# Expert fetches one at a time, query pieces loaded ahead, seven and then nine fetch buffers

## The chip, the cores and the metric

The kernel runs on one core of one Trainium2 chip. The metric is device time in microseconds (us) of one execution, the median of several. TensorE is PE, its weight loads are PEld, VectorE is DVE, ScalarE is ACT, GpSimd is POOL, and SyncE, which only issues loads and stores here, is SP. Each engine works through its own queue in order, and a queue whose head has to wait holds up everything behind it.

## The reference, cut to what matters

Two transformer blocks run over 256 tokens of width 1024. The first block is attention (a difference attention and a retention, side by side) and then a feed-forward layer of product-key experts; the second block follows and is not touched. What matters is the expert layer:

```python
def one_block(xb):                                    # 128 tokens; there are two such tiles
    q = (xb @ w_query).reshape(tb, 8, 2, 128)
    s = einsum('thpd,hpnd->thpn', q, sub_keys)        # 8 heads, 2 halves, 128 keys each
    top_s, top_i = top_k(s, 16)
    # all pairs of the two halves, 16 best pairs -> 16 expert numbers and gates a head
    best_s, pos = top_k(cand_s, 16)
    eid  = take_along_axis(cand_i, pos)
    gate = softmax(best_s)
    u = take(expert_down, eid)                        # rows of 1024
    act = gelu(einsum('thkd,td->thk', u, xb))
    v = take(expert_up, eid)                          # rows of 1024
    return einsum('thk,thkd->td', gate * act, v)
```

So each token fetches 128 experts (8 heads of 16), each a row of 1024 numbers for `u` and one of 1024 for `v`.

## The kernel before

`uv` in device memory holds the `u` row and the `v` row of each of the 16384 experts side by side. A fetch (line 753) is one indirect DMA from POOL: for one slot s of 128 it brings, for the 128 tokens of a tile, 128 rows of 8 KB, 1 MB in all. There are 2 x 128 fetches. A fetch buffer is a tile `uv` of the pool `up`; there are eight. For each fetch DVE forms the dot product of the `u` half with the normed token `xn` (line 756, to `dots`), ACT applies Gelu (759), multiplies by the gate (765) and spreads the result over a diagonal `dg` (767), and PE multiplies `dg` by the `v` half into two accumulators (770: two matmuls in the source, which run as four). Only then is the buffer free for a later fetch. `fetch` works in pairs: two fetches and two dots, then one Gelu over both, then the rest for the pair before in the source.

The expert numbers are found while the fetches run. `queries` multiplies by 16 pieces of `w_query` (512 KB each) and by the sub-keys `skT`; `picks` (its generator `choose` from line 632) does the two top-16 searches on DVE and one Exp on ACT for each unit of heads (line 680). Between fetches, `picking(time, t, h)` emits DVE steps until their estimated costs reach `time`; the table `due` forces a unit to be finished by a given slot. `behind()` keeps such DVE steps behind the dot of that slot in DVE's queue; it ties no other engine. `query(1)` or `memory(1)` emits half a head, or a piece of the memory block's weights, about every sixth slot.

A weight piece goes through `piece`: SP loads it (line 166, tile `raw`), ACT rounds it to `wh` (167), and DVE takes the rest `wl` (168). `raw`, `wh` and `wl` have three buffers each, in the pool `wp`, shared by all weights. So the load of a piece waits until DVE has done the `wl` of the piece three before, and its `wh` waits until PE is done with that piece.

The toolchain places instructions in each engine's queue by its own estimate of when they can run, so that a load or a rounding may stand ahead of its place in the source. Attention (`mix1`) lives in the pool `m1`, whose room the expert stage then reuses tile by tile; the expert stage opens `up2` when all queries are done. `skT` and `qT` lie in the pool `qp`, which closes then.

Of the kernel before, what the change touches and what calls it, by code (L numbers as in the profile page):

```python
# [15 lines left out]
OP = mybir.AluOpType  # L16
# [98 lines left out]
class K:  # L115
# [32 lines left out]
    def piece(self, src, shape, between=None):  # L148
# [3 lines left out]
        def t(tag, dt):  # L152
            x = self.wp.tile([128, 1024], dt, name=tag, tag=tag)
            x = x[:, :n]
            if len(shape) > 1:
                x = x.rearrange("p (a b) -> p a b", b=shape[-1]) if len(shape) == 2 else \
                    x.rearrange("p (a b c) -> p a b c", b=shape[1], c=shape[2])
            return x
# [152 lines left out]
    def mix1(self):  # L311
# [3 lines left out]
        with self.tc.tile_pool(name="m1", bufs=1, reuse_waits="tile") as mp:  # L315
# [90 lines left out]
            mix = M([128, 2, 1024], "mix")  # L406
            mT = (M([128, 8, 256], "mTh", F32R), M([128, 8, 256], "mTl", F32R))
# [7 lines left out]
            dif = mix[:, :, :512].rearrange("p t (h d) -> p t h d", d=128)  # L415
            ret = mix[:, :, 512:].rearrange("p t (h d) -> p t h d", d=128)
# [72 lines left out]
            fill(4)  # L489
            a = diff_turn(p)  # L490
# [19 lines left out]
            a = diff_turn(p)  # L510
            diff_out(3, a)
# [29 lines left out]
            def half(nb, k0):  # L541
# [4 lines left out]
                if k0:  # L546
                    self.squares(nb)
# [16 lines left out]
    def rope(self, v, g, half, cn, sn, M):  # L564
# [4 lines left out]
        a = M([128, 2, g, 64], "ropeA", bufs=1)[:, :, :, :2 * half]  # L569
        b = M([128, 2, g, 64], "ropeB", bufs=1)[:, :, :, :2 * half]  # L570
# [5 lines left out]
    def transposeN(self, x, nb, M, tag):  # L576

        nc = self.nc
        o = (M([128, nb, 256], tag + "h", F32R), M([128, nb, 256], tag + "l", F32R))
# [30 lines left out]
    def queries(self, pool, skT, sS):  # L610
# [3 lines left out]
        self.first_T([I["w_query"][b] for b in range(2)], two, self.pv("ffn_g", 0, 8))  # L614
        self.r = self.res_r()
        for h in range(8):
            qT = pool.tile([128, 2, 256], F32, name="qT", tag="qT", bufs=2)
            for i in range(2):
                o = two[i]
                if h:  # L620
                    o = self.pa([128, 256])
                    self.proj_T(self.hT, self.piece(I["w_query"][2 * h + i], [8, 128]), 8, o)
# [63 lines left out]
    def experts(self):  # L686
# [4 lines left out]
        with self.tc.tile_pool(name="p2", bufs=1, reuse_waits="tile") as p2, \  # L691
# [15 lines left out]
            xn = [P([1024], f"xn{t}") for t in range(2)]  # L707
            for t in range(2):
                nc.gpsimd.dma_start(xn[t], I["ffn_gr"].to_broadcast([128, 1024]))
# [8 lines left out]
            units = [(0, h, 1) for h in range(4)] + [(0, 4, 2), (0, 6, 2), (1, 0, 4), (1, 4, 4)]  # L718
# [21 lines left out]

            def fetch(t, acc):
# [3 lines left out]
                last = None  # L745
                for s in range(0, 130, 2):
                    new = None
                    if s < 128:
                        rows = []
                        dots = up.tile([128, 2], F32, name="dots", tag="dots", bufs=4)  # L750
                        for i in range(2):
                            x = up.tile([128, 2048], F32, name="uv", tag="uv", bufs=8)
                            nc.gpsimd.indirect_dma_start(x, None, I["uv"],  # L753
                                                         bass.IndirectOffsetOnAxis(ap=eids[:, s + i:s + i + 1], axis=0))
                            junk = self.junk([128, 1024], "junk", BF)
                            self.dot = nc.vector.scalar_tensor_tensor(junk, x[:, :1024], 1.0, xn[t], op0=OP.mult,  # L756
                                                                      op1=OP.mult, accum_out=dots[:, i:i + 1])
                            rows.append(x)
                        nc.scalar.activation(dots, dots, AF.Gelu, scale=self.r[:, t:t + 1])  # L759
                        new = s, rows, dots  # L760
                    if last:
                        s0, rs, ds = last
                        dg = up.tile([128, 2, 128], F32, name="dg", tag="dg", bufs=3)
                        for i in range(2):
                            nc.scalar.activation(ds[:, i:i + 1], ds[:, i:i + 1], AF.Copy,  # L765
                                                 scale=gates[:, s0 + i:s0 + i + 1])
                            nc.scalar.activation(dg[:, i], self.ident, AF.Copy, scale=ds[:, i:i + 1])  # L767
                        for i in range(2):
                            for d in range(2):
                                nc.tensor.matmul(acc[d], dg[:, i], rs[i][:, 1024 + 512 * d:1536 + 512 * d],  # L770
                                                 start=s0 + i == 0, stop=s0 + i == 127)
                    last = new
                    yield s
# [4 lines left out]
            due = {8: (0, 2), 24: (0, 3), 40: (0, 4), 56: (0, 6), 88: (0, 8), 120: (1, 4)}  # L778
            with self.tc.tile_pool(name="qp", bufs=1, reuse_waits="tile") as qp:
# [12 lines left out]
                for s in tile0:  # L792
                    with behind():
                        if s in (2, 6, 10) or s > 10 and s % 6 == 4:
                            query(1)
                            n += 1
                        picking(1500, 0, min(8, (n + 1) // 2))
# [4 lines left out]
                query.rest()  # L802
            with self.tc.tile_pool(name="up2", bufs=1, reuse_waits="tile") as up2:
                self.fg = up2.tile([128, 1024], F32, name="fgr")
                nc.sync.dma_start(self.fg, I["final_g"].to_broadcast([128, 1024]))
                self.xg = [up2.tile([128, 512], F32, name=f"xg{t}") for t in range(2)]
                for s in tile0:
                    with behind():
                        if s % 6 == 4:
                            self.memory(1)  # L810
                        picking(1500, 1, 8)
# [873 lines left out]
```

## Time and profile before

| | |
|---|---|
| median of 3 runs | 1339.29 us (1338.74 to 1340.62) |
| profiled execution, its own time | 1340.03 us |
| its span in the profile | 1338.0 us |
| mean granted TensorE clock | 0.960 of full speed |
| busy share of the span: PE, DVE, ACT, POOL | 88%, 70%, 47%, 24% |
| fetches `uv`, from first issue to last landing | 147.7 to 865.4 us |

The profiled execution's own time is 2.0 us over its span, and 0.7 us over the median. The profile puts a busy time, a count and an idle time with its releaser beside each group of instructions; a busy PE is not a PE at its peak, since matmuls are pipelined and their ends modelled. Device memory traffic is given as GB/s and as a busy share of the core's 16 DMA engines.

### The profile page before, as it was taken

Reading aid. Unit: us, or ns where it says so; the run is one execution under the profiler, and the core shown is the slowest. Engines: PE = TensorE matmul, PEld = TensorE weight load, DVE = VectorE, ACT = ScalarE, POOL = GpSimd, SP = SyncE. Lnnn points to the kernel's source line nnn. Section 1 sums busy time; section 2 is a strip of 40 time slices with the busy share of each in tenths; the row PEclk is TensorE's granted clock in tenths of the full one; section 3 lists DMA queues with packets and bytes.
Section 4 is the critical chain, followed back from the end, with each engine's and each line's share of the span. In section 5 each row is a group of like instructions: output and inputs, shape, how many; then the busy total and the mean of one; then the engine's idle time right before and its main releaser. Section 6 shows DMA issues by size and latency. Waiting matters only on the chain.

```text
span 1338.0 us, 16678 instructions
## 1 busy us (share of the span) xinstructions
PE 1171.0 (88%) x5430; PEld 807.6 (60%) x5430; DVE 936.2 (70%) x2188; ACT 633.4 (47%) x1501; POOL 315.5 (24%) x283
## 2 busy tenths in 40 slices
PE   7999688979688988879877777789999999999996
PEld 5877554545344444344432223279987898999996
DVE  6888678575777776555545455478987885988887
ACT  6676434333332423423322222257877575655554
POOL 0020334434244544334443333110001000000001
PEclk9999798989899999989999999999999999999998
DMA  7645599999999999999999999846334464656562
GB/s 261 227 140 174 231 361 400 406 371 420 373 371 395 406 420 410 359 411 422 421 422 422 420 422 420 342 130 190 122 106 127 131 215 142 192 188 181 185 188 95
DMA packets 81769, 388.61 MB, mean 290 GB/s; under 512 B 8196, under 2 KB 10324, under 8 KB 48788
## 3 DMA queue, kind: packets, MB, share of 16 engines
q0 software_dynamic: 37408, 270.56, 49.6%
q1 hardware_dynamic: 42260, 114.38, 26.3%
q10 hardware_dynamic: 2016, 2.62, 0.5%
q8 instruction: 43, 0.70, 0.2%
q14 instruction: 42, 0.34, 0.1%
HBM read 384.38 MB, written 3.15 MB: 290 GB/s over the span
## 4 chain that ended last, share of the span: by engine, by line
PE 38%; DMA 31%; issue 13%; DVE 9%; POOL 5%; ACT 3%; POOLq 0%; SPq 0%; ACTq 0%; DVEq 0%
DMA uv<-in_uv_dram,eid 27%; PE pa L173 5%; PE pa L174 5%; PE pa L175 5%; POOL uv L753 5%; PE pb L173 4%; PE pa L1514 4%; PE pb L175 4%; PE pb L174 4%; DVE junk L756 3%; PE pb L770 2%; DVE wl L168 2%; DMA raw<-in_w_query_dram 1%; DMA raw<-in_w_mem_k_dram 1%; DMA raw<-in_w_in_dram 1%
## 5 line engine op out<-in xcount | busy, mean ns | idle before, releaser
L770 PE MATMUL pb<-uv,dg 128*128 128x512 f32 x1024 | 495.5, 632 | 100.5 <-ACT dg L767 100.3
L756 DVE SCALAR_TENSOR_TENSOR junk<-uv,xn 128x1024 bf16<-128x1024 f32 x256 | 313.4, 1224 | 239.8 <-DMA uv<-in_uv_dram,eid 229.3
L770 PEld LDWEIGHTS pb<-uv,dg 128*128 128x128 f32 x1024 | 198.4, 202 | 358.2 <-issue 198.6
L753 POOL DMA_INDIRECT uv<-in_uv_dram,eid x256 | 286.5, 1119 | 451.4 <-PE pb L770 303.3
L167 ACT ACTIVATE wh<-raw 128x1024 fp32r<-128x1024 f32 (+3 forms) x203 | 211.9, 1047 | 367.1 <-DMA raw<-in_w_mem_v_dram 51.4
L168 DVE TENSOR_TENSOR wl<-raw,wh 128x1024 fp32r<-128x1024 f32 (+3 forms) x203 | 246.7, 1219 | 60.2 <-ACT wh L167 59.7
L759 ACT ACTIVATE dots<-dots,rs_y 128x2 f32<-128x2 f32 x128 | 37.3, 292 | 240.1 <-DVE junk L756 236.8
L173 PE MATMUL pb<-nTh,wh 128*128 128x256 f32 x416 | 117.7, 283 | 0.0
L174 PE MATMUL pb<-nTl,wh 128*128 128x256 f32 x416 | 117.7, 283 | 0.0
L175 PE MATMUL pb<-nTh,wl 128*128 128x256 f32 x416 | 117.4, 283 | 0.0
L767 ACT ACTIVATE dg<-cvt,dots 128x128 f32<-128x128 f32 x256 | 86.9, 386 | 0.0
L175 PE MATMUL pa<-nTh,wl 128*128 128x256 f32 x256 | 78.0, 305 | 5.6 <-DVE wl L168 5.6
L173 PE MATMUL pa<-nTh,wh 128*128 128x256 f32 x256 | 78.2, 306 | 4.5 <-ACT wh L167 4.4
L174 PEld LDWEIGHTS pb<-nTl,wh 128*128 128x128 f32 x416 | 79.5, 191 | 1.0
L173 PEld LDWEIGHTS pb<-nTh,wh 128*128 128x128 f32 x416 | 79.5, 191 | 1.0
L175 PEld LDWEIGHTS pb<-nTh,wl 128*128 128x128 f32 x416 | 79.5, 191 | 0.0
L1538 POOL TENSOR_TENSOR xs<-xr,ng 128x512 f32<-128x512 f32 x4 | 5.1, 1290 | 313.9 <-DVE xr L1536 313.9
L174 PE MATMUL pa<-nTl,wh 128*128 128x256 f32 x256 | 73.6, 288 | 0.0
L173 PE MATMUL pa<-wh,nTh 128*128 128x512 f32 (+1 forms) x144 | 58.2, 412 | 9.8 <-ACT wh L167 9.0
L765 ACT ACTIVATE dots<-dots,gate 128x1 f32<-128x1 f32 x256 | 61.5, 286 | 4.0
L174 PE MATMUL pa<-wl,nTh 128*128 128x512 f32 (+1 forms) x144 | 58.1, 403 | 3.2 <-DVE wl L168 3.2
L175 PE MATMUL pa<-wh,nTl 128*128 128x512 f32 (+1 forms) x144 | 57.5, 400 | 0.0
(460 smaller groups left out, 1895.2 us busy)
## 6 DMA issues: line engine op xcount, KB each, us to landing
raw<-in_w_ffn_up_dram SPq DMA_DIRECT2D x44, 512.0 KB, 3.7
raw<-in_w_out_dram SPq DMA_DIRECT2D x24, 512.0 KB, 3.7
raw<-in_w_in_dram SPq DMA_DIRECT2D x23, 512.0 KB, 4.7
raw<-in_w_ffn_down_dram SPq DMA_DIRECT2D x22, 512.0 KB, 3.6
raw<-in_w_query_dram SPq DMA_DIRECT2D x16, 512.0 KB, 7.1
raw<-in_w_xbc_dram SPq DMA_DIRECT2D x16, 512.0 KB, 4.1
uv<-in_uv_dram,eid POOLq DMA_INDIRECT x256, 11.1
raw<-in_w_mem_v_dram SPq DMA_DIRECT2D x8, 512.0 KB, 10.4
```

What stands on the lines that cost most here:

```text
L167: nc.scalar.activation(h[:, s], raw[:, s], AF.Copy)
L168: self.wl = nc.vector.tensor_sub(lo[:, s], raw[:, s], h[:, s])
L173: mm(out, a[0], b[0], start=start, stop=False)
L174: mm(out, a[0], b[1], start=False, stop=False)
L175: mm(out, a[1], b[0], start=False, stop=stop)
L753: nc.gpsimd.indirect_dma_start(x, None, I["uv"], bass.IndirectOffsetOnAxis(ap=eids[:, s + i:s + i + 1], axis=0))
L756: self.dot = nc.vector.scalar_tensor_tensor(junk, x[:, :1024], 1.0, xn[t], op0=OP.mult, op1=OP.mult, accum_out=dots[:, i:i + 1])
L759: nc.scalar.activation(dots, dots, AF.Gelu, scale=self.r[:, t:t + 1])
L765: nc.scalar.activation(ds[:, i:i + 1], ds[:, i:i + 1], AF.Copy, scale=gates[:, s0 + i:s0 + i + 1])
L767: nc.scalar.activation(dg[:, i], self.ident, AF.Copy, scale=ds[:, i:i + 1])
L770: nc.tensor.matmul(acc[d], dg[:, i], rs[i][:, 1024 + 512 * d:1536 + 512 * d], start=s0 + i == 0, stop=s0 + i == 127)
L1514: nc.tensor.matmul(acc[d][t], a[x][:, t * 128:(t + 1) * 128], w[y][:, d], start=b == 0 and x + y == 0, stop=b == 21 and x == 1)
```

## The change

Room: the two scratch tiles of the rotary step and the output `mix` become one tile `mix`, and the transposed `dq` and `dk` share the tiles `mTh` and `mTl` with the later transposed `mix`. A new pool `qraw` of four 4 KB buffers a partition is open from before attention until the queries are done; the `raw` of query pieces 3 to 15 goes there, and `wp` keeps the rest.

Fetches: `fetch` handles one slot at a time (own dot, own Gelu, one `dg`), with seven buffers in `up` until the queries are done and two more in `up2` from then on. `dots` has six buffers and `dg` four, both for one fetch each.

The rest: the second `xn` moves from a POOL load before the fetches to an SP load into `up2`; tile 1's picks go in four units of two heads (before: two units of four), with due slots to match; `picking` gets half the time at each of twice as many slots; and `squares(1)`, four ACT instructions for the second half of the residual, moves from the end of `mix1` to behind the first two query pieces.

```diff
-    def piece(self, src, shape, between=None):
+    def piece(self, src, shape, between=None, pool=None):
...
-            x = self.wp.tile([128, 1024], dt, name=tag, tag=tag)
+            x = (pool if pool and tag == "raw" else self.wp).tile([128, 1024], dt, name=tag, tag=tag)
...
-                if k0:
+                if k0 and not nb:
                     self.squares(nb)
...
-        a = M([128, 2, g, 64], "ropeA", bufs=1)[:, :, :, :2 * half]
-        b = M([128, 2, g, 64], "ropeB", bufs=1)[:, :, :, :2 * half]
+        ab = M([128, 2, 1024], "mix").rearrange("p i (t g d) -> p i t g d", t=2, d=64)[:, :, :, :, :2 * half]
+        a, b = ab[:, 0], ab[:, 1]
...
-        o = (M([128, nb, 256], tag + "h", F32R), M([128, nb, 256], tag + "l", F32R))
+        o = M([128, 2 * nb, 256], {"dqT": "mTh", "dkT": "mTl"}.get(tag, tag), F32R)
+        o = (o[:, :nb], o[:, nb:])
...
         self.first_T([I["w_query"][b] for b in range(2)], two, self.pv("ffn_g", 0, 8))
+        self.squares(1)
...
-                    self.proj_T(self.hT, self.piece(I["w_query"][2 * h + i], [8, 128]), 8, o)
+                    self.proj_T(self.hT, self.piece(I["w_query"][2 * h + i], [8, 128], pool=self.qraw if 2 * h + i > 2 else None), 8, o)
...
-            xn = [P([1024], f"xn{t}") for t in range(2)]
-            for t in range(2):
-                nc.gpsimd.dma_start(xn[t], I["ffn_gr"].to_broadcast([128, 1024]))
+            xn = [P([1024], "xn0"), None]
+            nc.gpsimd.dma_start(xn[0], I["ffn_gr"].to_broadcast([128, 1024]))
...
-            units = [(0, h, 1) for h in range(4)] + [(0, 4, 2), (0, 6, 2), (1, 0, 4), (1, 4, 4)]
+            units = [(0, h, 1) for h in range(4)] + [(0, 4, 2), (0, 6, 2)] + [(1, h, 2) for h in (0, 2, 4, 6)]
...
+            uvs = [up] * 7
+            count = [0]
...
-                for s in range(0, 130, 2):
...
+                for s in range(128):
+                    pool = uvs[count[0] % len(uvs)]
+                    count[0] += 1
+                    x = pool.tile([128, 2048], F32, name="uv", tag="uv", bufs=uvs.count(pool))
+                    nc.gpsimd.indirect_dma_start(x, None, I["uv"],
+                                                 bass.IndirectOffsetOnAxis(ap=eids[:, s:s + 1], axis=0))
+                    w = up.tile([128, 1], F32, name="dots", tag="dots", bufs=6)
+                    junk = self.junk([128, 1024], "junk", BF)
+                    self.dot = nc.vector.scalar_tensor_tensor(junk, x[:, :1024], 1.0, xn[t], op0=OP.mult, op1=OP.mult,
+                                                              accum_out=w)
+                    nc.scalar.activation(w, w, AF.Gelu, scale=self.r[:, t:t + 1])
+                    nc.scalar.activation(w, w, AF.Copy, scale=gates[:, s:s + 1])
+                    dg = up.tile([128, 128], F32, name="dg", tag="dg", bufs=4)
+                    nc.scalar.activation(dg, self.ident, AF.Copy, scale=w)
+                    for d in range(2):
+                        nc.tensor.matmul(acc[d], dg, x[:, 1024 + 512 * d:1536 + 512 * d], start=s == 0, stop=s == 127)
                     yield s
...
-            due = {8: (0, 2), 24: (0, 3), 40: (0, 4), 56: (0, 6), 88: (0, 8), 120: (1, 4)}
+            due = {8: (0, 2), 24: (0, 3), 40: (0, 4), 56: (0, 6), 88: (0, 8), 120: (1, 2)}
...
-                        picking(1500, 0, min(8, (n + 1) // 2))
+                        picking(750, 0, min(8, (n + 1) // 2))
...
+            self.qraw_cm.__exit__(None, None, None)
             with self.tc.tile_pool(name="up2", bufs=1, reuse_waits="tile") as up2:
+                xn[1] = up2.tile([128, 1024], F32, name="xn1")
+                nc.sync.dma_start(xn[1], I["ffn_gr"].to_broadcast([128, 1024]))
+                uvs += [up2] * 2
...
+                due = {22: 4, 54: 6, 86: 8}
...
-                        if s == 54:
-                            picking(1e6, 1, 8)
+                        if s in due:
+                            picking(1e6, 1, due[s])
...
         with tc.tile_pool(name="mk", bufs=1) as k.mk:
+            k.qraw_cm = tc.tile_pool(name="qraw", bufs=4, side="right")
+            k.qraw = k.qraw_cm.__enter__()
             k.mix1()
```

## Rows read from the trace of the kernel before

**Rows 1.** The page: DMA rate in 40 equal slices of the span.
```profile
GB/s 261 227 140 174 231 361 400 406 371 420 373 371 395 406 420 410 359 411 422 421 422 422 420 422 420 342 130 190 122 106 127 131 215 142 192 188 181 185 188 95
```

**Rows 2.** Windows of the expert stage: stretch, length, busy times, granted clock, DMA share, GB/s.
```profile
147.73:154.22 6.49, 4.44 (x21) 4.44 (x22) 1.99 (x2) 0.00 (x0) 5.27 (x5) 0.60 0.61 213
154.22:330.00 175.78, 145.87 (x515) 81.90 (x515) 119.99 (x359) 69.40 (x194) 69.76 (x60) 0.92 0.98 394
330.00:528.00 198.00, 164.38 (x447) 83.07 (x446) 149.74 (x469) 67.48 (x197) 84.57 (x69) 0.91 0.99 396
528.00:696.00 168.00, 138.22 (x398) 67.02 (x397) 86.13 (x139) 54.35 (x183) 69.05 (x65) 0.94 0.99 407
696.00:865.50 169.50, 127.85 (x284) 51.66 (x283) 84.27 (x136) 44.88 (x165) 60.43 (x62) 0.99 1.00 416
```

**Rows 3.** Windows: two after a piece that had landed early, and one late.
```profile
300.00:320.00 20.00, 19.19 (x81) 11.58 (x80) 9.47 (x16) 7.19 (x20) 9.52 (x8) 1.00 1.01 419
320.00:340.00 20.00, 15.82 (x56) 8.22 (x54) 10.23 (x29) 5.19 (x17) 7.28 (x7) 1.00 1.01 419
...
760.00:780.00 20.00, 14.95 (x34) 5.90 (x33) 10.01 (x17) 5.44 (x20) 8.55 (x8) 1.00 1.02 422
```

**Rows 4.** Waits of ACT from 154 to 330 us: total us, times, longest.
```profile
ACT wh L167 <- DMA raw<-in_w_query_dram: 41.9, 5, 12.4
...
ACT wh L167 <- DMA raw<-in_w_mem_v_dram: 9.3, 1, 9.3
```

**Rows 5.** Waits of ACT from 330 to 696 us.
```profile
ACT wh L167 <- DMA raw<-in_w_mem_v_dram: 42.1, 4, 11.0
ACT wh L167 <- DMA raw<-in_w_mem_k_dram: 34.8, 5, 8.9
...
ACT wh L167 <- DMA raw<-in_w_latq_dram: 15.4, 2, 7.9
```

**Rows 6.** Timelines of DVE, SP, ACT and PE around one query piece.
```profile
260.48 1.22 DVE L168 TENSOR_TENSOR wl<-raw,wh 128x1024 fp32r<-128x1024 f32 x1
...
261.76 0.33 SPq L166 DMA_DIRECT2D raw<-in_w_query_dram  x1
...
270.35 1.06 ACT L167 ACTIVATE wh<-raw 128x1024 fp32r<-128x1024 f32 x1 [8.36 <-DMA raw<-in_w_query_dram]
...
271.73 1.11 PE L629 MATMUL pb<-skT,qT 128*128 128x128 f32 x4 [4.41 <-ACT qT L623]
```

**Rows 7.** Timeline of ACT at the first memory piece, which had landed.
```profile
305.20 1.06 ACT L167 ACTIVATE wh<-raw 128x1024 fp32r<-128x1024 f32 x1 [6.91 <-PE pa L174]
```

**Rows 8.** Waits of POOL from 154 to 330 us, and the fetches' time to landing.
```profile
POOL uv L753 <- PE pb L770: 83.4, 34, 10.2
...
DMA to landing us min/median/max: 5.5/11.1/17.8
```

**Rows 9.** Timelines of DVE, ACT and PE at the last pair of fetches.
```profile
863.04 1.23 DVE L756 SCALAR_TENSOR_TENSOR junk<-uv,xn 128x1024 bf16<-128x1024 f32 x1 [1.29 <-DMA uv<-in_uv_dram,eid]
...
865.45 1.23 DVE L756 SCALAR_TENSOR_TENSOR junk<-uv,xn 128x1024 bf16<-128x1024 f32 x1 [1.18 <-DMA uv<-in_uv_dram,eid]
...
866.72 0.29 ACT L759 ACTIVATE dots<-dots,rs_y 128x2 f32<-128x2 f32 x1 [3.54 <-DVE junk L756]
...
867.43 0.68 ACT L767 ACTIVATE dg<-cvt,dots 128x128 f32<-128x128 f32 x2
...
867.87 3.70 PE L770 MATMUL pb<-uv,dg 128*128 128x512 f32 x8 [1.24 <-ACT dg L767]
```

**Rows 10.** Window of the first queries, up to the first fetch.
```profile
119.00:147.70 28.70, 24.76 (x171) 22.42 (x169) 22.75 (x86) 18.29 (x34) 0.00 (x0) 1.00 0.44 137
```

**Rows 11.** One tile's instructions: last reads of `mTl`; reads of `skT`.
```profile
L175 PE MATMUL pa<-wh,mTl x32: 387/389/398, 105.0 to 127.8; 128*128 128x512 f32 x32
...
L629 PE MATMUL pb<-skT,qT x64: 270/275/582, 137.7 to 343.2; 128*128 128x128 f32 x64
```

**Rows 12.** One line's instructions: table loads before the Exp of the picks.
```profile
L680 ACT ACT_TABLE_LOAD x8: 1283/1283/1283, 143.5 to 517.3; - x8
```

More of the change, by code (lines that the diff above doesn't have):

```diff
@@ L405, in mix1 @@
                 nc.scalar.activation(dec[:, h], tmp, AF.Exp)
-            mix = M([128, 2, 1024], "mix")
-            mT = (M([128, 8, 256], "mTh", F32R), M([128, 8, 256], "mTl", F32R))
             def fillers():
@@ L412, in mix1 @@
             fill = Filler(fillers())
-            dif = mix[:, :, :512].rearrange("p t (h d) -> p t h d", d=128)
-            ret = mix[:, :, 512:].rearrange("p t (h d) -> p t h d", d=128)
             def diff_scores(h):
@@ L489, in mix1 @@
             fill(4)
+            mix = M([128, 2, 1024], "mix")
+            dif = mix[:, :, :512].rearrange("p t (h d) -> p t h d", d=128)
+            ret = mix[:, :, 512:].rearrange("p t (h d) -> p t h d", d=128)
             a = diff_turn(p)
@@ L510, in mix1 @@
             a = diff_turn(p)
+            mT = (M([128, 8, 256], "mTh", F32R), M([128, 8, 256], "mTl", F32R))
             diff_out(3, a)
@@ L744, in fetch @@
                 eids = self.eid[t].rearrange("p h k -> p (h k)")
-                last = None
-                for s in range(0, 130, 2):
[L747 to L772, printed above, removed]
@@ L793, in experts @@
                     with behind():
-                        if s in (2, 6, 10) or s > 10 and s % 6 == 4:
+                        if s in (3, 7, 11) or s > 11 and s % 6 == 5:
                             query(1)
                             n += 1
-                        picking(1500, 0, min(8, (n + 1) // 2))
+                        picking(750, 0, min(8, (n + 1) // 2))
                         if s in due:
@@ L808, in experts @@
                     with behind():
-                        if s % 6 == 4:
+                        if s % 6 == 5:
                             self.memory(1)
-                        picking(1500, 1, 8)
+                        picking(750, 1, 8)
                         if s in due:
@@ L823, in experts @@
                         if s > 10:
-                            picking(1500, 1, 8)
-                        if s == 54:
-                            picking(1e6, 1, 8)
+                            picking(750, 1, 8)
+                        if s in due:
+                            picking(1e6, 1, due[s])
                         if s % 6 == 2 and 10 < s < 100:
```

## Prediction

> **What bounds the kernel now.** I read the page's rate by slices first. It stands near 420 GB/s in the slices of about 500 to 840 us, and below that, unevenly, in those of about 160 to 500 us [rows 1]. So the expert stage is bound by its fetches, but not all of it runs at the rate that the fetches can have. Then the windows: late in the stage, with no weights and no picks left, the rate is 422 GB/s [rows 3]. I take that as what the DMA can give here, and ask of each stretch how much of its length it lost against it [rows 2]:
>
> - 147.7 to 154.2, the first fetch on its way: 6.49 x (1 - 213/422) = 3.2 us
> - 154.2 to 330, queries and fetches: 175.78 x (1 - 394/422) = 11.7 us
> - 330 to 528, memory pieces and the last picks: 198 x (1 - 396/422) = 12.2 us
> - 528 to 696, the rest of the memory pieces: 168 x (1 - 407/422) = 6.0 us
> - 696 to 865.5: 169.5 x (1 - 416/422) = 2.4 us
>
> Together 35.5 us. Nothing in the stage can give back more, unless bytes leave it. In the same rows PE is busy 83%, DVE 68% and ACT 39% of 154 to 330 us, and 83%, 76% and 34% of the time to 528: no engine is full [rows 2].
>
> Why does the DMA idle, then? The waits of POOL say that fetches stood 83.4 us for a buffer, released by PE [rows 8]. Why is PE late? The waits of ACT: it stood before the rounding `wh` of a piece for 41.9 + 9.3 us in the first stretch and for 42.1 + 34.8 + 15.4 = 92.3 us in the next two, each time for the piece's load, some 8 us at a time [rows 4, 5]. One case shows the chain: DVE ends `wl` of a piece at 261.7 us, which frees a `raw`; SP issues the next load at 261.76; ACT, whose queue has that piece's `wh` next, stands 8.36 us until 270.35; Gelu and `dg` of the landed fetches are behind it, and PE's next work starts at 271.73, idle for 4.41 us [rows 6]. No buffer comes free in between. A natural experiment stands beside it: the first memory piece had landed when ACT came to it. ACT still stood, 6.91 us, but for PE to release a `wh` buffer [rows 7], and PE was at work: 300 to 340 us ran at 419 GB/s, with PE busy 35.0 of 40 us [rows 3]. So the wait for a load costs DMA time and the wait for PE hardly does.
>
> **The change part by part.** The sum is made against the profiled execution's 1340.0 us (1338.0 span and 2.0 around it), which is 0.7 above the median.
>
> *Query pieces.* With four `raw` buffers of their own, a query piece's load is issued when DVE ends `wl` of the piece four before, while its `wh` still goes by the piece three before: a whole piece earlier, six fetches or some 15 us before ACT needs it. The waits of 41.9 us go, and so does one of memory pieces, whose three `wp` buffers lie free from query piece 2 on. What is late next is PE's release of `wh`, as in the natural experiment: at 419 of 422 GB/s the 164 us left of this stretch would lose 1.2 us. Two things are added there. One buffer fewer: bounds 0 and 25 us (a rival, below); I take half a fetch, 1.2 us (1 MB at 422 GB/s is 2.485 us). And the two new buffers lie in the room of `qraw`, which the last `wl` frees; that is queued behind the dot of slot 59, so it ends some 2.5 us after that dot starts (1.27 to the dot's release of ACT [rows 9], 1.22 for `wl` [rows 6]). The fetch that waits for it stands at POOL's head with all later fetches behind it. With the shortest landing, 5.5 us [rows 8], it lands 8.0 us after that dot, against two fetches, 5.0 us, at full rate: at most 3.0 us lost, nothing if POOL had the room sooner. I take 2.5. Left of 11.7 us: 1.2 + 1.2 + 2.5 = 4.9. Gain **6.8 us**.
>
> *Single fetches, nine buffers.* At the last pair the dots start at 863.04 and 865.45, Gelu at 866.72, `dg` at 867.43, and the eight matmuls take 867.87 to 871.57 [rows 9]. The first buffer is free half of 3.70 us after the matmuls start: 6.7 us after its dot starts; the second after 6.1. Singly, no step takes longer: 1.27 from dot to Gelu, 0.71 to `dg` (with two gate multiplies, of which one will be left), 0.44 to the matmuls and 1.85 for half of them make 4.3. A buffer comes back 2.4 or 1.8 us sooner, 2.1 in the mean. A Gelu of one column has no row; I took the 0.29 us of two columns, its upper bound, which is within the 0.71. From slot 60 on there is also one buffer more than before, 2.5 us of landing. The memory pieces keep their waits (only the first ones come earlier): 18.2 us lost for 11 waits, 1.65 us a wait, against 4.6 us of new slack. The mean is covered; the waits reach 11.0 us, and DVE's picks add their own delays, so I leave a third, 6.0 us. Gain **12.2 us**. From 696 us I take 0.5 of 2.4 us. At the end, the last fetch's matmuls end 1.8 us sooner after it lands. Gain **2.3 us**.
>
> *What moves bytes.* The loads of pieces 3 to 6 came before the first fetch already; now piece 7's does too: 0.524 MB, 1.2 us out of the bound stretch. The second `xn`, as large, comes into it. Zero in sum. Issued as early as in attention, four loads cost 2.1 MB, 5.0 us at most, and are hidden: the DMA share just before the fetches is 0.44 [rows 10].
>
> *What is priced at nothing.* ACT gets 128 more Gelus, at most 37 us, under its waits: it is busy 236 of 711 us of the stage [rows 2]. DVE gets the fixed part of two more `choose` passes, where a quarter of its time is idle. The shared tiles could hold up attention, or a late-freed `mTl` could lie under `skT`: it is last read at 127.8 us, and `skT`, 1 MB, is first read at 137.7 [rows 11]; the shortest landing of 1 MB, 5.5 us [rows 8], would leave 4.4 us of cover, and beyond it the price is us for us. Moving `squares(1)` off ACT can bring the first fetch forward by no more than PE is idle before it, 3.9 of 28.7 us [rows 10]; between 0 and that I take nothing, as PE's queue has the scores before the first picks. Four units instead of two for tile 1 mean two more Exps, each with a table load before it and one back to Gelu: 4 x 1.283 = 5.1 us of ACT [rows 12]. Bounds 0 and 5.1; I take 0, since ACT's idle time covers it.
>
> The Trainium skill speaks against that last edit: "ScalarE: Activation LUTs", section "Table sets: the hidden batching unit", asks for calls to be batched by set, and its rules budget about 2.7 us a switch. By that budget the four would be 10.8 us and the forecast some 1329; the trace has 1.283 a load.
>
> Sum: 6.8 + 12.2 + 2.3 = 21.3; 1340.0 - 21.3 = 1318.7, and against the median **1318**.
>
> **The rivals.**
> *The wait only changes its name.* ACT still stands 6 to 7 us a query piece, for PE, and with a buffer fewer that costs what the load did: nothing from the queries, half from the memory pieces. 6.1 + 2.3 = 8.4, 1331. For it: the 6.91 us [rows 7]. Against it: 419 GB/s around it [rows 3].
> *All of it comes back.* Every loss but the first stretch's goes: 32.3 + 1.8 = 34.1, 1305. For it: the engines' idle time. Against: the 80% that DVE would then need from 330 to 528 us (149.7 of 185.8) [rows 2].
> *Seven buffers starve the queries* (the slower side). Sixty fetches in 175.8 us are 2.93 us each, with eight buffers a turn of 23.4 us. If waits and not the pairs make that turn, and it stays, seven give 3.35 us each: 25 us more, against 12.2 + 2.3 gained later: +11, 1350. It decides if the turn stays over 7 x (175.8 + 14.5)/60 = 22.2 us. For it: POOL's 83.4 us for buffers [rows 8]. Against: the turn is long because of ACT's waits, which the same change removes.
> *The table switches are paid.* ACT's 5.1 us come on top: 1323.
>
> **How the numbers follow.** The forecast with its own range, 1308 to 1326 (the losses left halved or grown by half): 0.55. Name only: 0.15; all back: 0.08; starved: 0.11; switches paid: 0.06; gains and losses that cancel: 0.05. The range that leaves out no more than 2 in 10 runs from the all-back case to just under the starved one: 1305 to 1338. About 0.2%, 2.7 us, can be told from no change here. Faster 0.55 + 0.15 + 0.08 + 0.06 = 0.84, same 0.05, slower 0.11.
>
> **What would show it.** Right: no ACT wait for `w_query` loads at line 167 once fetches run; POOL's wait for PE below half of 83 us; 405 GB/s or more in each stretch from the second on; the last landing near 845 us and about 4.3 us from it to the last matmul's end. Wrong: a first fetch after 149 us (the room); ACT waits for `wh` put down to PE with PE idle (name only); the query stretch longer than 176 us (starved); a gap of the DMA at slot 60 above 3 us.

## The result, and the profile after

The changed kernel takes **1318.09 us** (median of four runs, 1317.63 to 1318.94), the kernel before 1339.95 on the same chip: a ratio of 0.9835, 95% interval 0.9818 to 0.9852. The forecast was 1318, with 1305 to 1338 around it. The profiled execution took 1317.63 us, with a span of 1315.9 against 1338.0.

The page's rate by slices first, which answers to [rows 1]:

```profile
GB/s 265 285 126 163 213 419 420 420 420 421 418 414 408 420 421 348 377 423 421 422 422 420 422 422 419 260 164 166 144 95 137 139 220 141 186 181 188 183 186 96
```

The uneven part from 160 to 500 us is level now. One hole is left, of two slices (348 and 377) at about 490 to 560 us. To price both the level part and the hole, I cut the stage where the work changes: at the dots of slot 0 and slot 60 of the first tile (queries up to there), of the second tile's first fetch (128), of fetch 146 (behind the change of tiles) and at the last dot (255). The windows of the changed kernel between these dots, with columns as in [rows 2]:

```profile
155.10:317.70 162.60, 147.98 (x526) 79.78 (x525) 121.69 (x365) 88.06 (x225) 68.08 (x61) 0.98 1.01 421
317.70:510.40 192.70, 163.75 (x463) 82.80 (x461) 154.52 (x519) 90.99 (x236) 89.36 (x71) 0.94 1.01 417
510.40:563.50 53.10, 38.05 (x104) 17.90 (x104) 26.61 (x47) 23.06 (x70) 20.95 (x20) 0.92 0.87 349
563.50:845.20 281.70, 230.57 (x551) 93.16 (x551) 141.79 (x226) 113.32 (x343) 104.73 (x103) 0.98 1.01 417
```

The kernel before, cut at its own dots of the same fetches:

```profile
154.30:332.10 177.80, 147.89 (x520) 82.72 (x520) 122.09 (x372) 70.03 (x195) 70.62 (x61) 0.92 0.98 394
332.10:530.00 197.90, 164.28 (x459) 84.17 (x458) 148.63 (x458) 66.85 (x194) 84.26 (x67) 0.91 0.99 395
530.00:582.00 52.00, 41.67 (x115) 19.66 (x114) 27.38 (x47) 18.62 (x63) 21.76 (x21) 0.93 0.94 381
582.00:865.50 283.50, 222.40 (x550) 97.01 (x550) 142.03 (x226) 80.61 (x285) 107.09 (x106) 0.97 1.01 417
```

So the four stretches changed by -15.2, -5.2, +1.1 and -1.8 us. The first dot is 0.8 us later, and from the last dot's start to the last matmul's end it is 4.4 us instead of 6.1 [rows 9], -1.75. The sum is -22.05, and the spans differ by 22.1: all of it lies between the first dot and the end of the fetches.

### The profile page after: what moved, and what is told of

It is laid out like the page before. It is cut to its first block, busy times and chain, and to the rows that moved or that the text cites. A ratio compares the mean times of both kernels' runs of the same rounds, so it can differ in the third digit from the quotient of the medians.

```text
span 1315.9 us, 16960 instructions
## 1 busy us (share of the span) xinstructions
PE 1173.4 (89%) x5430; PEld 796.1 (61%) x5430; DVE 940.7 (71%) x2242; ACT 712.7 (54%) x1635; POOL 313.6 (24%) x282
## 4 chain that ended last, share of the span: by engine, by line
PE 41%; DMA 35%; DVE 9%; issue 6%; ACT 6%; POOL 3%; SPq 0%; POOLq 0%; DVEq 0%; ACTq 0%
DMA uv<-in_uv_dram,eid 28%; PE pb L764 5%; PE pa L173 5%; PE pa L174 5%; PE pa L175 5%; PE pa L1511 4%; PE pb L173 4%; PE pb L174 4%; PE pb L175 4%; DMA raw<-in_w_mem_v_dram 3%; POOL uv L753 3%; DVE junk L757 3%; DVE wl L168 2%; DMA raw<-in_w_in_dram 2%; ACT wh L167 1%
## 5 line engine op out<-in xcount | busy, mean ns | idle before, releaser
L764 PE MATMUL pb<-uv,dg 128*128 128x512 f32 x1024 | 502.6, 628 | 98.3 <-ACT dg L762 96.9
L764 PEld LDWEIGHTS pb<-uv,dg 128*128 128x128 f32 x1024 | 188.6, 197 | 367.6 <-ACT dg L762 195.9
L759 ACT ACTIVATE dots<-dots,rs_y 128x1 f32<-128x1 f32 x256 | 74.4, 290 | 238.5 <-DVE junk L757 238.2
L762 ACT ACTIVATE dg<-cvt,dots 128x128 f32<-128x128 f32 x256 | 102.7, 401 | 9.3 <-PE pb L764 1.3
L760 ACT ACTIVATE dots<-dots,gate 128x1 f32<-128x1 f32 x256 | 75.2, 294 | 9.6 <-ACT dots L759 1.8
L173 PE MATMUL pa<-wh,nTh 128*128 128x512 f32 (+1 forms) x144 | 57.6, 408 | 10.4 <-ACT wh L167 9.6
```

The costliest lines, as they stand in the source:

```text
L173: mm(out, a[0], b[0], start=start, stop=False)
L759: nc.scalar.activation(w, w, AF.Gelu, scale=self.r[:, t:t + 1])
L760: nc.scalar.activation(w, w, AF.Copy, scale=gates[:, s:s + 1])
L762: nc.scalar.activation(dg, self.ident, AF.Copy, scale=w)
L764: nc.tensor.matmul(acc[d], dg, x[:, 1024 + 512 * d:1536 + 512 * d], start=s == 0, stop=s == 127)
```

## The experiments

Every kernel is read by the same cut. The loss of a stretch is worked out as in the prediction, its length times (1 - rate/422). "Ratio" is to the kernel before, run on the same chip. The medians are of all executions of a kernel, while the stretches and losses are those of its one profiled execution. That was the longest of six for "changed, pairs" (1331.51 us) and "changed, shared query places" (1333.69), so their losses may be somewhat too large.

| kernel | median us | ratio, 95% interval | dots 0-60: us, loss | 60-128 | 128-146 | 146-255 | losses |
|---|---|---|---|---|---|---|---|
| before | 1339.95 | 1 | 177.8, 11.8 | 197.9, 12.7 | 52.0, 5.1 | 283.5, 3.4 | 33.0 |
| changed | 1318.09 | 0.9835, 0.9818-0.9852 | 162.6, 0.4 | 192.7, 2.3 | 53.1, 9.2 | 281.7, 3.3 | 15.2 |
| before, single fetches | 1323.47 | 0.9870, 0.9847-0.9894 | 167.2, 2.4 | 194.0, 5.5 | 54.2, 7.8 | 282.2, 3.3 | 19.0 |
| changed, pairs | 1326.63 | 0.9888, 0.9863-0.9914 | 167.3, 4.8 | 193.5, 6.0 | 52.4, 7.3 | 283.5, 4.0 | 22.1 |
| changed, shared query places | 1329.74 | 0.9912, 0.9893-0.9932 | 176.8, 11.3 | 191.6, 1.4 | 53.5, 8.0 | 282.6, 4.0 | 24.7 |
| changed, seven all through | 1325.82 | 0.9896, 0.9875-0.9917 | 162.5, 0.8 | 196.5, 9.3 | 52.6, 6.5 | 288.0, 8.2 | 24.8 |
| changed, six, then nine | 1322.44 | 0.9862, 0.9839-0.9885 | 172.6, 2.5 | 185.7, 5.7 | 51.9, 7.3 | 283.3, 3.4 | 18.9 |
| changed, xg on DVE | 1317.76 | 0.9833, 0.9812-0.9853 | 162.7, 0.4 | 192.7, 2.7 | 46.5, 0.1 | 284.1, 8.1 | 11.3 |
| changed, xg of tile 0 on DVE | 1314.57 | 0.9808, 0.9784-0.9832 | 162.5, 0.4 | 192.6, 2.7 | 46.6, 0.1 | 284.1, 8.1 | 11.3 |
| the same, skT and xn0 held | 1311.13 | 0.9790, 0.9771-0.9809 | 162.6, 0.8 | 192.9, 2.7 | 46.5, 0.1 | 284.3, 8.1 | 11.7 |
| before, xg of tile 0 on DVE | 1337.10 | 0.9973, 0.9957-0.9989 | 175.9, 10.8 | 197.7, 11.2 | 48.3, 1.9 | 284.9, 4.1 | 28.0 |

**Theory and rivals.** The theory on record: ACT's waits for query loads cost DMA time, so the places of their own give the query stretch back; single handling and nine buffers give back the later ones. The rivals: the wait only changes its name, and seven buffers starve the queries. The profile after raised a third question, the hole at the change of tiles.

**Single fetches alone.** The kernel before, with the changed kernel's way of handling a fetch and nothing else of the change. Half of `picking`'s time at each of twice as many slots goes with it, here and the other way round in the run with pairs below; what that does by itself was not tried. The edit, cut:

```diff
-                for s in range(0, 130, 2):
+                for s in range(128):
...
-                        dots = up.tile([128, 2], F32, name="dots", tag="dots", bufs=4)
+                    w = up.tile([128, 1], F32, name="dots", tag="dots", bufs=6)
```

> The kernel before with one edit: each fetch has its own dot, Gelu, gate multiply, dg and two matmuls, and the matmuls are no longer a pair late. Eight buffers, query pieces through the three shared places. Theory (pairs hold buffers 2.1 us too long): the last matmul comes 1.8 us sooner, and the memory stretches get back about the share 2.1/4.6 of the 12.2 us that the prediction gave to single fetches and the ninth buffer together: 5.6 us; the query stretch, whose waits are ACT's, little. 1339.5 - 7 to 10: 1330 to 1333, with the waits of ACT for w_query loads as before, some 40 us. Rival (only the number of buffers and the query places matter): the end's 1.8 us alone, 1337 to 1338.

It took 1323.47 us, 17.3 below the 1340.74 of before on that chip: almost four fifths of the whole gain, and far more than either expectation. The query stretch lost 2.4 us instead of 11.8. ACT's waits in that stretch, in total, number and longest:

```profile
ACT wh L167 <- DMA raw<-in_w_query_dram: 37.6, 8, 6.3
ACT wh L167 <- PE pa L174: 11.7, 2, 6.7
```

The waits for the loads are nearly all still there (41.9 us before [rows 4]), and the DMA ran at 416 GB/s beside them. A wait of ACT for a load is no loss by itself; it is one when the fetches in flight run out before it ends.

**Query pieces through the shared places again.**

```diff
-                    self.proj_T(self.hT, self.piece(I["w_query"][2 * h + i], [8, 128], pool=self.qraw if 2 * h + i > 2 else None), 8, o)
+                    self.proj_T(self.hT, self.piece(I["w_query"][2 * h + i], [8, 128]), 8, o)
```

> The changed kernel, but all query pieces load through the three shared places again; the four places of their own stay allocated and empty, so buffers, fetches and hand-over are as in the changed kernel. Theory (ACT's waits for the loads cost DMA time): the waits of 40 to 50 us come back in ACT's view between the first fetch and 330 us, and with seven buffers the time is 7 to 10 us longer than that of the changed kernel: 1325 to 1328. Rival (the wait only changes its name): within 2 us of the changed kernel, 1316 to 1320.

1329.74 us: 11.65 over the changed kernel (10.3 by the two ratios), more than expected, and nearly all in the query stretch (176.8 us, 395 GB/s). ACT's waits there:

```profile
ACT wh L167 <- DMA raw<-in_w_query_dram: 35.5, 7, 6.6
ACT wh L167 <- PE pa L174: 11.4, 2, 5.8
ACT wh L167 <- DMA raw<-in_w_mem_v_dram: 7.8, 1, 7.8
```

They are nearly the waits of the run before, and here the stretch loses 11.3 us instead of 2.4. What differs in how fetches are handled is one buffer, seven for eight; the changed kernel's other moves (the shared tiles, `squares(1)`, the units of picks) stand in this run too and were not undone. The rival of the changed name is out, since the wait for PE costs next to nothing. In the changed kernel the waits for PE were these, at 421 GB/s:

```profile
ACT wh L167 <- PE pa L174: 24.6, 10, 9.3
```

**Pairs in the changed kernel.**

```diff
-                for s in range(128):
+                for s in range(0, 130, 2):
...
```

> The changed kernel with fetches handled in pairs as before: two dots to a Gelu, matmuls one pair late; places of their own for query pieces, seven and then nine buffers stay. Theory (slack: a pair holds each buffer 2.1 us longer, which is nearly what a buffer brings, whatever ACT waits for): dot 0 to dot 60 takes 168 to 178 us, the memory stretch 2 to 4 us more, the end 1.8 us more: 1325 to 1335. Rival (pairs cost only where ACT waits for loads of query pieces, and these are early now): 1320 to 1322. The rival of the prediction (seven buffers starve the queries, with pairs): 1345 or more.

1326.63 us, inside the slack theory's range; the query stretch, at 167.3 us, is a little below it. Its first dot was also late, at 160.5 us, in that longest of its executions, and no run says why; what pairs cost between the dots is the losses' difference, 22.1 - 15.2 = 6.9 us, and 1.75 at the end. Seven buffers with pairs do not starve the queries: at the rival's 3.35 us each, 60 fetches would be 201 us.

**Seven buffers all through; six, then nine.**

```diff
-                uvs += [up2] * 2
```

> The changed kernel without the two buffers that lie in the freed room: seven all through. Theory (buffers are the slack against the waits for memory pieces): single handling gives 2.1 us of slack and the missing eighth buffer takes 2.5 us, so the stretch from 330 to 700 us loses again what it lost before, 10 to 12 us more than the changed kernel: 1328 to 1330. Rival (with single handling the buffers no longer bind): 1318 to 1320.

```diff
-            uvs = [up] * 7
+            uvs = [up] * 6
...
-                uvs += [up2] * 2
+                uvs += [up2] * 3
```

> The changed kernel with six buffers instead of seven while queries are computed, and three instead of two in the freed room, so that nine stand again from slot 60 on. Theory (a buffer is 2.5 us of slack, and the changed kernel has little left in this stretch, in which ACT still stands up to 9.3 us for PE): dot 0 to dot 60 takes 165 to 172 us, against 162.6 with seven, and the time is 1321 to 1327. Rival (at 420 GB/s the seventh buffer did nothing): 162 to 164 us and 1317 to 1319. The rival of the prediction (the turn of a buffer stays and its number sets the pace): 162.6 x 7/6 = 190 us and about 1345.

Seven all through: 1325.82, 7.7 over the changed kernel (8.2 by the ratios); it lost 9.3 us in the memory stretch and 8.2 in the last one, where the changed kernel lost 2.3 and 3.3. The theory said 10 to 12, so the buffers do bind there and its size was too large: at the change of tiles this kernel lost 2.7 us less (below).

Six, then nine: 1322.44, inside the theory's range, but dot 60, 10 us later, is a poor sign of it. Dot 60 waits there for the first fetch into the freed room; in the changed kernel that is dot 61, behind the cut. From the timelines of DVE, six buffers and then the changed kernel:

```profile
329.08 1.23 DVE L757 SCALAR_TENSOR_TENSOR junk<-uv,xn 128x1024 bf16<-128x1024 f32 x1 [9.10 <-DMA uv<-in_uv_dram,eid]
...
326.94 1.22 DVE L757 SCALAR_TENSOR_TENSOR junk<-uv,xn 128x1024 bf16<-128x1024 f32 x1 [7.07 <-DMA uv<-in_uv_dram,eid]
```

Up to dot 59 the six took 160.2 us and the seven 159.4. What six cost in this stretch is some 2 us of idle DMA, nearly all at 300 to 312 us (315, 373 and 387 GB/s in its windows of 4 us). Another 3.4 us were lost from dot 60 to 128, with nine buffers standing; the cause is open. So this run doesn't show what a buffer is worth. The pace of the turn is refuted: 8 buffers turned in 177.8 x 8/60 = 23.7 us before, 7 in 19.0, 6 in 17.3. A buffer's turn shrinks with their number.

**The hole at the change of tiles.** The timeline of POOL in the changed kernel (start, length, idle before and its releaser):

```profile
506.78 0.94 POOL L753 DMA_INDIRECT uv<-in_uv_dram,eid  x1 [0.31 <-issue]
522.91 1.28 POOL L860 TENSOR_TENSOR xg<-xr,fgr 128x512 f32<-128x512 f32 x1 [15.19 <-ACT dots L760]
524.35 0.97 POOL L753 DMA_INDIRECT uv<-in_uv_dram,eid  x1 [0.16 <-issue]
...
530.63 1.10 POOL L753 DMA_INDIRECT uv<-in_uv_dram,eid  x1 [0.30 <-issue]
540.48 1.30 POOL L860 TENSOR_TENSOR xg<-xr,fgr 128x512 f32<-128x512 f32 x1 [8.74 <-ACT dots L760]
541.91 0.97 POOL L753 DMA_INDIRECT uv<-in_uv_dram,eid  x1
```

And DVE just ahead of the first of the two multiplies:

```profile
520.94 1.22 DVE L757 SCALAR_TENSOR_TENSOR junk<-uv,xn 128x1024 bf16<-128x1024 f32 x1 [1.44 <-DMA uv<-in_uv_dram,eid]
...
522.09 0.68 DVE L852 TENSOR_TENSOR xr<-xr,pb 128x512 f32<-128x512 f32 x1
```

`joined` hands POOL a multiply of 1.3 us that needs DVE's `xr` of line 852, and that stands behind the dot of the fetch at which `joined` is written. POOL runs up to nine fetches ahead of that dot. So it comes to the multiply long before it can run, and issues nothing behind it until DVE has caught up: all fetches in flight land, and the DMA runs dry. More buffers don't help; the further POOL is ahead, the longer it stands. With single fetches it stood at the two multiplies together 5.0 us with seven buffers all through, 18.0 with eight and 23.9 here with nine; with pairs 10.4 with eight and 13.3 with nine. (The 6.5 us that the kernel with seven lost in this stretch are then not these stands alone.) (The releaser named, ACT's `dots`, had long been done; it was `xr`.)

```diff
-        nc.gpsimd.tensor_mul(self.xg[t], xr[:, t, c], self.fg[:, c])
+        nc.vector.tensor_mul(self.xg[t], xr[:, t, c], self.fg[:, c])
```

> The changed kernel, but the multiply that makes xg in joined runs on DVE and not on POOL, where it stands in the queue ahead of later fetches. Theory (head of the queue): the two gaps between fetches of 17.6 and 11.3 us at about 507 to 542 us go, and with them the 9 us that 520 to 560 us lost against 420 GB/s: 1309 to 1311. Rival (the gap comes from the end of the first tile's sum and the transposes on PE, whatever engine multiplies): 1316 to 1319, with a gap of the same length and another releaser.

The hole went: dots 128 to 146 took 46.5 us, at 421 GB/s. The time did not move: 1317.76. The theory had the place and the rival the time; what happened stood in neither. The lead over the changed kernel, read at the same instructions of both traces, was 6.8 us at the dot of fetch 146, of which 0.3 stood at the first dot, 4.4 at the last dot, and 0.65 from about 884 us to the end. Two losses had taken its place.

The first lies at the last fetches. The windows of the next kernel (multiply on DVE for the first tile alone), which has the same last stretch, at 832 to 840 us:

```profile
832.00:834.00 2.00, 1.50 (x4) 0.49 (x3) 0.80 (x1) 0.97 (x3) 0.00 (x0) 1.00 0.63 262
834.00:836.00 2.00, 1.49 (x4) 0.49 (x3) 0.79 (x3) 0.99 (x3) 0.00 (x0) 1.00 0.16 66
836.00:838.00 2.00, 1.56 (x4) 0.38 (x2) 0.88 (x2) 0.99 (x3) 0.00 (x0) 1.00 0.06 25
838.00:840.00 2.00, 1.98 (x4) 0.68 (x4) 1.23 (x2) 0.59 (x2) 0.00 (x0) 1.00 0.06 25
```

A DMA share of 0.06 is one engine in sixteen, and 25 GB/s is about a sixteenth of 422. For 4 us one DMA engine alone finishes its part of the last fetches, while the dots still wait for landings: in the trace the packets of 8 KB follow one another there, 0.31 us each, and never two at once. In the changed kernel the fall was steeper (0.92, 0.39, 0.02 in 2-us windows from 840 us on). Its hole had let that engine catch up; the windows of the changed kernel in the hole show one engine at work while the others stand:

```profile
520.00:522.00 2.00, 2.00 (x6) 0.84 (x5) 1.06 (x1) 0.56 (x2) 0.00 (x0) 1.00 0.18 74
522.00:524.00 2.00, 2.00 (x6) 0.87 (x5) 0.77 (x3) 1.60 (x5) 1.09 (x1) 1.00 0.06 25
524.00:526.00 2.00, 2.00 (x8) 1.04 (x7) 0.00 (x0) 0.00 (x0) 1.53 (x3) 1.00 0.04 16
```

The second lies behind the stage. The windows of the kernel with all of xg on DVE:

```profile
870.00:874.00 4.00, 0.73 (x4) 0.42 (x3) 3.81 (x2) 2.04 (x3) 3.01 (x1) 0.83 0.01 4
874.00:878.00 4.00, 4.00 (x18) 3.90 (x19) 1.90 (x4) 0.30 (x1) 0.00 (x0) 0.50 0.68 223
```

PE stood 3.17 us for DVE's `wl` there, which was slow beside a copy on POOL (last section), and then ran at a granted clock of 0.50, the lower of the two levels (1.2 GHz), in the next 4 us. The second tile's multiplies on DVE had changed the order of work behind the last fetch, so that PE had no other work meanwhile; on POOL they stand where it has no fetch left to issue.

**Only the first tile's multiply on DVE.**

```diff
-        nc.gpsimd.tensor_mul(self.xg[t], xr[:, t, c], self.fg[:, c])
+        (nc.gpsimd if t else nc.vector).tensor_mul(self.xg[t], xr[:, t, c], self.fg[:, c])
```

> As the run before with the multiply of xg on DVE, but only for the first tile, whose multiply stands among the fetches; the second tile's, after the last fetch, is on POOL as in the changed kernel. Theory (the lead of 4.4 us at the last dot was lost behind it: DVE's longer queue, and an idle PE followed by the lower granted clock at 874 to 878 us): the lead stays, 1313 to 1315. Rival (the lead is taken by what comes after in any case): 1317 to 1319.

1314.57, as expected; from the last dot to the end of the span it is 470.7 us again, as in the changed kernel (474.5 with both on DVE). Once more, beside the changed kernel on one chip:

> The changed kernel once more, as a reference on the same chip as the three beside it: 1317 to 1319.

> The kernel with the first tile's multiply on DVE once more, beside the changed kernel: 3 to 5 us less than that, 1313 to 1315. If the first reading was chance, within 1 us of it.

1317.77 (0.9841, 0.9821 to 0.9861) and 1313.19 (0.9800, 0.9781 to 0.9820): 4.6 us less. The intervals just miss each other, and the first reading, against the changed kernel's earlier runs, gave 3.6 us by the ratios.

**The same edit in the kernel before.**

> The kernel before with one edit: the first tile's multiply of xg on DVE instead of POOL. Theory (the multiply at the head of POOL's queue stops the fetches at the change of tiles in the kernel before as well): dots 128 to 146 take 46 to 48 us instead of 52.0, and the time is 4 to 6 us less than before, 1334 to 1337. Rival (with pairs and eight buffers the stop is hidden by losses that come anyway): 1338 to 1341.

1337.10, 2.6 below the 1339.74 of before: less than the theory's 4 to 6, more than the rival's; dots 128 to 146 took 48.3 us. The stop was there all the time and lost less: POOL stood 2.38 and 8.04 us at the two multiplies in the kernel before, with eight buffers and pairs.

**The loads that the shared tiles delay.** In the changed kernel `xn0` and `skT` are issued at 113.7 and 114.3 us, not at 93.9 and 101.9: their room comes free later. ACT's timeline there, with the wait for the last w_out piece, which SP had issued at 116.17:

```profile
116.91 1.06 ACT L167 ACTIVATE wh<-raw 128x1024 fp32r<-128x1024 f32 x1 [2.53 <-DMA raw<-in_w_out_dram]
123.01 1.06 ACT L167 ACTIVATE wh<-raw 128x1024 fp32r<-128x1024 f32 x1 [5.04 <-DMA raw<-in_w_out_dram]
```

A first attempt to hold them asked only for an order behind `wl`, on DVE:

```diff
+                    with self.tc.issue_after(self.wl.ins):
+                        nc.gpsimd.dma_start(skT[:, b], I["skT"][:, b])
```

> As the kernel with the first tile's multiply on DVE, and the loads of xn0 and skT are issued only after the wl of the last w_out piece, so that they don't run beside that piece's load. Theory (that load took 6.4 us instead of 3.6 beside them, and made the first fetch 1.5 us late): first fetch at 147.5 to 148.2 us, and 1 to 1.5 us less than the kernel without the hold: 1312 to 1313.5. Rival (skT or xn0 is late in its place): first fetch at 149 us or later, no gain or a loss.

It tells nothing: POOL issued the loads at 114.1 and 114.7 us as before (1315.06 us, ratio 0.9814, 0.9792 to 0.9837). The second puts a reader of `wl` into POOL's own queue:

```diff
+            hold = nc.gpsimd.tensor_copy(self.sm([128, 1], F32, "hold", 1), self.lo[:, 0, 0:1])
+            with self.tc.issue_after(hold.ins):
```

> As the kernel with the first tile's multiply on DVE, and POOL first copies one column of the last w_out piece's wl, so that the loads of xn0 and skT behind it in its queue can't start before that wl exists (the hold of the run before stood on another engine and held nothing: the loads were issued at 114 us as before). Theory (these loads beside the w_out piece's made the first fetch late): that piece lands within 4.5 us of its issue, first fetch at 146.5 to 148 us, and 1 to 2 us less than without the hold: 1312 to 1313.5. Rival (skT, needed at 137 us, now lands too late): first fetch after 149 us and the same or a longer time.

The timelines of ACT and POOL in it:

```profile
120.42 1.06 ACT L167 ACTIVATE wh<-raw 128x1024 fp32r<-128x1024 f32 x1 [2.07 <-DMA raw<-in_w_out_dram]
...
124.70 1.08 POOL L778 DMA_DIRECT2D skT<-in_skT_dram  x2
147.12 1.15 POOL L756 DMA_INDIRECT uv<-in_uv_dram,eid  x1 [21.33 <-DVE eid L678]
```

The piece is rounded 3.7 us after its load's issue at 116.73, against 6.7 in the kernel beside it without the hold; the first fetch goes out at 147.12 instead of 148.4; and the time is 1311.13 us, 2.1 below that kernel and below the theory's range. The delay by the loads is seen. Its price stays rough, as the intervals of the two overlap, and in the two profiles 1.0 of 1.9 us lies behind the last dot, where the hold has no part. It is the fastest of all, 28.6 us below the kernel before.

## Why the prediction was right, and where it was not

The time was right to 0.1 us, but its terms were not: two errors made up for two others, so that the closeness was luck. The size and the way of the change were forecast; where it would come from was not.

- **The query stretch**: 6.8 predicted; the loss fell by 11.4, to 0.4. The three prices left in it (waits for PE, a seventh buffer, the hand-over at slot 60: 4.9 us) came to next to nothing. Behind dot 60 DVE stood 7.07 us for a landing, but the windows of 4 us around it have 411 to 424 GB/s: no gap. The prediction had the fetch into the freed room at POOL's head with all later ones behind it. By the trace's semaphores, dot 61 waits for the fetch that POOL issued at 317.66, just behind the last `wl`, and the three issued before it, at 309.49 to 313.72, are those of later slots.
- **Its reason**: this is the step that failed. The prediction gave that stretch's loss to ACT's waits for loads, and single handling to the later stretches. But single handling alone takes 9.4 of the 11.8 us while the waits stay. The 2.1 us that it took for a pair were read at the last pair, where nothing else waits, and hold there: from the start of a dot to the end of its last matmul it is 6.6 us before and 4.4 with single fetches, in the mean of slots 72 to 121 of the second tile. In the query stretch the same mean is 12.4 us before and 8.8 with single fetches alone, 3.6 less. Three things draw on one account, the time that the fetches in flight can cover: a pair holds a buffer 2.1 to 3.6 us longer, a buffer is 2.5 us by the estimate, and a load wait draws from it as long as it lasts, 6.3 us at most singly and 12.4 with pairs. Pairs with eight buffers and single fetches with seven, both with the load waits, lost about the same in this stretch (11.8 and 11.3): there a pair costs some of what a buffer brings. That the sums agree so well is partly chance, as they were lost at other slots (5.8 and 0.4 us in the first 20). The terms could not be added; the first edit that fills the account gets the credit.
- **330 to 696 us**: 12.2 predicted. By the dots' cut, 10.4 came back before the change of tiles, and then 4.1 were lost at it. That hole was in the rates of before (410, 359 and 411 GB/s in the slices from 502 to 602 us [rows 1]). The prediction passed over it where it read those slices as near 420, and put the loss down to the memory pieces. With the last stretch's 0.1 that makes 6.4.
- **Bytes**: nothing in sum predicted. Three mem_v pieces went out before the first fetch, at 127.7 to 133.5 us, where the prediction had only piece 7: 286.3 MB moved between the first and the last dot before and 284.8 after, 3.6 us less.
- **The end**: 1.8 predicted, 1.75 measured; 4.36 us from a dot to its last matmul's end, against 4.3.
- **The front**: nothing predicted, with 4.4 us of cover for `skT`. The load had its cover; what it cost was the w_out piece beside it, as the held loads above show. The first fetch went out at 149.3 us, past the announced 149, and the first dot was 0.8 us late. In the profile of the same kernel's second run they come at 147.9 and 154.0, the dot 0.3 us earlier than before: POOL's load of `iota`, far ahead of any of this, is at 94.38 us in the one, 93.23 in the other and 93.17 before. So those 0.8 us are the spread of executions.

Sum of losses, bytes, front and end: 17.8 + 3.6 - 0.8 + 1.75 = 22.35, against 22.1 of the span (the rates are rounded). One slip in the prediction's own range: 16.0 us of losses left, halved, give 1310 and not 1308.

The table loads before Exp and the dots' Gelu went from 16 to 20, of 1283 ns each, as predicted. Their price was not tried by itself. That the stretch with the four more of them ran at 417 GB/s leaves little. By the Trainium skill's budget ("ScalarE: Activation LUTs", section "Rules for kernel authors") they would have been four of some 2.7 us, an estimate that no row shows.

Two signs were badly chosen. POOL's wait for buffers released by PE was to fall below half of 83.4 us [rows 8], and is 53.1 us in 31 waits: with a full DMA POOL must wait for each buffer, so this wait measures fullness, not loss. And 405 GB/s in each long stretch hid one of 53 us at 349. The sign that there be no wait of ACT for query loads once fetches run held: the view of 154 to 330 us has none left.

## What to carry to other kernels

Waits that draw on the same cover don't add: before giving a stall's price to the engine that shows it, ask how long the transfers in flight would last, and undo one edit at a time to see which refills the account. A compute instruction in the queue of the engine that issues the loads stops them for as long as that engine runs ahead; deeper buffering made it worse here. Removing a hole in a transfer-bound stage can give back only part of it: here 9.1 us came back and 4.8 were lost at the end, as the slowest DMA engine had used the hole to catch up.

## What the runs showed of the hardware

**One DMA engine finishes last.** With no hole left, one engine worked alone for some 4 us after the others (rows above, share 0.06). Why it is behind is open. The Trainium skill says that two of the sixteen are usually slower in traces than the others ("DMA: Bandwidth & Descriptors", section "Latency and other measured facts"); the trace here fits that, with two packets at a time for a short while before the last engine is alone, but doesn't name the engines.

**DVE beside a POOL copy.** Behind the stage, DVE's two subtracts of 128x768 took 4.78 us while POOL copied `kT` for 3.60; one alone took 0.95. From the timelines of DVE and POOL in the changed kernel:

```profile
867.93 0.95 DVE L168 TENSOR_TENSOR wl<-raw,wh 128x768 fp32r<-128x768 f32 x1
...
873.36 4.78 DVE L168 TENSOR_TENSOR wl<-raw,wh 128x768 fp32r<-128x768 f32 x2 [0.76 <-ACT wh L167]
...
872.59 3.60 POOL L1026 COPY kT<-krT 32x4096 f32<-32x4096 f32 x1 [19.50 <-issue]
```

The copy ends at 876.19, and two subtracts of 0.95 us behind it would end at 878.09; they end at 878.14. So they did next to nothing while the copy ran. The Trainium skill tells of a port pair that DVE and GpSimd lock against each other for a whole instruction ("SBUF — State Buffer", section "SBUF: two separate sides"), with which this agrees. That PE then can stand and its clock fall, as in the run above with 4.77 us for the same two subtracts, is the price that these traces add.
